# Token sums kept in fp32, weight sums regrouped, down products reordered and norm spreads put later in a one-core decoder trunk on Trainium2

## The chip, the cores and the metric

The kernel runs on one core of one Trainium2 chip. A core has TensorE (matrix products into the eight banks of PSUM), VectorE (DVE), ScalarE (ACT), GpSimd (POOL) and SyncE (SP), and 16 DMA engines that all queues share. The metric is the device time of one launch in microseconds, as the median over repeated runs.

## The reference

One layer of a decoder trunk over x of shape (1, 2048, 1024) in float32, conditioned by c:

```python
sh1, sc1, g1, sh2, sc2, g2 = jnp.split(mod, 6, axis=-1)      # mod = silu(c) @ w_ada + b_ada
h = rms_norm(x) * (1.0 + sc1) + sh1
x = x + g1 * token_mixer(h, ...)      # retention | HGRN2 | GLA heads, one in- and one out-projection
h = rms_norm(x) * (1.0 + sc2) + sh2
x = x + g2 * conv_ffn(h, ...)         # u = causal depthwise conv (width 3) of h @ w_up; (silu(gate) * val) @ w_down
return rms_norm(x) * final_gain
```

The token mixers run in chunks with a carried state; d_ff is 2816. Inputs are drawn from normal distributions, and some of the gains and biases are scaled up.

## The kernel before, in words

Every large product is made in float32 accuracy from two parts. `split` (L970 to L974) casts a tile to a rounded part `hi` on ScalarE (L972) and subtracts to get the remainder `lo` on VectorE (L973); `split3` (L239 to L243) then issues three matmuls, hi by hi, hi by lo and lo by hi.

The channel mixer works on pairs of blocks of 512 tokens, `s` = 0 and 1. Its two matrix products are done block by block in a 2 x 2 scheme of seven products instead of eight. They are numbered 1 to 7: each takes a sum or difference of weight blocks (the "weight sums") and one of token blocks (the "token sums"). In the up stage, `up_first` issues products 1, 2, 6, 5 and 7 of one feature tile `f` (22 of them), and `up_second` products 4 and 3 of the tile before, after product 1 of the next. X holds the running sum over 1, 6, 7 and 4, Y holds 2, Z holds 5 and then 3. In the down stage `down_stage` runs the seven products in an order of their own; each is 11 steps of 12 matmuls over four banks. X again gathers 1, 6, 7 and 4, and 2, 5 and 3 go to other banks. After a product its banks are read out into the residual rows y (L1421); once rows are whole, their squares go into a sum for the final norm (`sumsq`, L334 to L340).

Stages in order of time: a start-up; the mixers for four token blocks b = 0 to 3 (each with seven units of heads: h0, g, h1, h2, h3, r0, r1), with the output projection of block b interleaved into block b + 1; the up stage for s = 0, its down stage, and the same for s = 1.

Order of work. TensorE's instructions are issued in program order, which is written by hand: a small clock (`Clock`) counts TensorE's planned microseconds, and `clock.at(us, fn)` puts a later piece of work into the order once that much planned time has gone by. The other engines, and the DMA queues of SP and POOL, are put in order at compile time by a list scheduler that goes by priority (`tc.high_priority(offset=...)` moves a piece forward). On the chip each engine's queue is worked off in order.

Names that matter here:

- `rstd` (L312 to L332) makes a norm: matmuls with ones (the tile `ss..`, L319), three Newton steps on VectorE (L153 to L158), and after `gap` planned microseconds a broadcast by matmul (the tile `bc..`, L329), copied by ScalarE (L330).
- `norm1_stat(b)` squares block b's tokens and starts such a norm with gap 8.0; it is called ahead of unit h3 of the block before, and its result is used after that block's last unit.
- `weight_sums` (L872 to L886) makes weight sums from raw weights in the mixers, as background work, and stores them in DRAM (`sums`): all 11 of the down stage, and those of the odd tiles of the up stage, one job at a time from the list `jobs`, the last in block 3.
- `up_weights(s, f)` supplies the operands A of tile f. Where `sums` has them they are loaded into tiles `s` (tag t2s, two buffers) and split. Otherwise it loads the raw weights, makes four sums on VectorE (L1165, L1166, L1169, L1172), splits them, and stores them for the second pair.
- `early_sums(k)` runs in block 3, after the second to fifth unit: it makes the token sums for products 5, 6, 7 and 4 of pair 0, splits each (tile `eo`), and stores both parts in DRAM (`made`). It draws its tiles from the ring `xy` (four buffers of 1024 columns), from which the residual rows of the output projection and `weight_sums` draw too. `fetch_made(B, i)` loads both parts by DMAs on POOL's queue (L1025) into the operand tiles B.
- `out_finish` ends the last output projection: residual rows `x1` (L919), their squares, the norm n2, and the stores of x1 and of the normalised block.
- `down_norm(s, h, ...)` makes the final norm of half h, then scales the rows (L1286) and stores them by POOL. In pair 0 two of the first half's rows lie in t2s tiles. `last_product` replaces the last product of pair 1 and ends the kernel.
- PSUM rings: `acc` (four banks), `lev` (two), `late` (two).

Of the kernel before, what the change touches and what calls it, by code (L numbers as in the profile page):

```python
# [100 lines left out]
def trunk(ctx, tc, xT, vecs, cvec, cst, rope, msk, wada, win, walow, wgla, wout, wup, wdown, out):  # L101
# [30 lines left out]
    def late(name):  # L132
        return pt.tile([P, 512], F32, tag="tl", name=name, bufs=NTL)
# [199 lines left out]

    def sumsq(acc, x, k, name, sl=slice(0, TB), first=None):  # L334
        if k == 0 if first is None else first:
            S.activation(acc[:, sl], x[:, sl], AF.Square)
        else:
            sq = late(f"sq{name}{k}")
            S.activation(sq[:, sl], x[:, sl], AF.Square)
            V.tensor_tensor(acc[:, sl], acc[:, sl], sq[:, sl], op=ALU.add)  # L340
# [139 lines left out]
    def norm1_stat(b):  # L480
        acc = new_acc(f"n1_{b}")
        for k in range(KD):
            x = tmp(f"x{b}_{k}")
            nc.sync.dma_start(x[:], xT[b, :, k, :])
            sumsq(acc, x, k, f"n1_{b}_")
        bc1[b] = new_bc1(b)
        clock.at(22.0, rstd(acc, f"n1_{b}", bc1[b][:], lambda: done.add(("n1", b)), gap=8.0))

# [511 lines left out]
    def early_sums(k):  # L1000

        t1, t2 = (px.tile([P, SB], F32, tag="xy", name=f"es{k}_{i}", bufs=4) for i in range(2))
        b11, b12, b21, b22 = t1[:, 0:TB], t1[:, TB:SB], t2[:, 0:TB], t2[:, TB:SB]
        for dst, src in ((b11, h2d[0, k]), (b12, h2d[1, k]), (b22, h2d[1, k + 4]), (b21, h2d[0, k + 4])):
            nc.sync.dma_start(dst, src[:])

        def op(i, src):
            t = px.tile([P, SB], F32R, tag="xy", name=f"eo{k}_{i}", bufs=4)
            split(src, t[:, 0:TB], t[:, TB:SB])
            made[i, k] = pdr.tile([P, SB], F32, tag=f"made{i}_{k}", name=f"made{i}_{k}")  # L1010
            nc.sync.dma_start(made[i, k][:], t[:].bitcast(F32))
        V.tensor_tensor(b11, b12, b11, op=ALU.subtract)
        op(5, b11)
        V.tensor_tensor(b11, b22, b11, op=ALU.subtract)
        op(6, b11)
        V.tensor_tensor(b12, b22, b12, op=ALU.subtract)
        op(7, b12)
        V.tensor_tensor(b21, b21, b11, op=ALU.subtract)
        op(4, b21)

    def fetch_made(B, i):
        for k in range(4):
            B[i, k] = hc_tile(f"B0_{i}_{k}")
            for j, t in enumerate(B[i, k]):
                G.dma_start(t.bitcast(F32), made[i, k][:, j * TB:(j + 1) * TB])  # L1025

# [9 lines left out]
    for hi, lo, raw, i in W0.values():  # L1036
        keep(f"i{i}l", lo[:])
    jobs = [job for k in range(NF // 2) for job in (("d", k), ("u", 2 * k + 1))]
    for b in range(NB):
# [103 lines left out]

    def up_weights(s, f, A=None, rv=None, rg=None):

        nm = f"{s}_{f}"
        op = lambda i, src: up_op(A, s, f, i, src)
        half = lambda n, j: raw_half(wup[2 * f + n][:, 512 * j:512 * j + 512], f"r{n}{j}_{nm}")
        if A is None:
            A = {}  # L1150
            rv = half(0, 0), half(0, 1)
            op(1, rv[0])
            op(2, rv[1])
        s1, s2, s3, s4 = (t2s(f"s{i}_{nm}") for i in range(4))
        if ("u", f) in sums:
# [6 lines left out]
            return A  # L1162
        rg = rg or (half(1, 0), half(1, 1))
        d = new_sums(("u", f))
# [54 lines left out]
    def up_first(s, f, A, B, before, begun=None):  # L1219
        nm = f"{s}_{f}"  # L1220
        X, Y = begun or (acc_ps("X" + nm), lev_ps("Y" + nm))
        Z = acc_ps("Z" + nm)
# [38 lines left out]
    INTO = {1: [(0, 0)], 2: [(0, 0)], 6: [(1, 0)], 5: [(1, 0), (1, 4)], 7: [(1, 4)], 4: [(0, 4)], 3: [(1, 0)]}  # L1261
    WHOLE = {2, 7, 4, 3}

# [15 lines left out]
    def down_norm(s, h, y, acc, bc, bank=None):  # L1279
# [11 lines left out]
        def then():  # L1291
            for i, m in enumerate(order):
                clock.at(2.0 * i, lambda m=m: scale(m))
        clock.at(7.0 if h else 10.0, rstd(acc, f"n3_{b}", bc[:], then, bank=bank, gap=4.5 if h else 8.0))

# [16 lines left out]
    def last_product(s, y, acc):  # L1312
# [56 lines left out]
        whole = slice(0, TB)  # L1369
        banks = [lev_ps(f"dL{p}") for p in range(2)]  # L1370
        run([b[:] for b in banks], (0, 1), whole, M512)
# [12 lines left out]
    def down_stage(s, between):  # L1384
# [4 lines left out]
        accs = [px.tile([P, TB], F32, tag=t, name=f"n3a{s}_{h}", bufs=1) for h, t in enumerate(("ssacc", "bc2"))]  # L1389
        for i in (1, 2, 6, 5, 7, 4, 3):  # L1390
            if i == 3 and s == NSB - 1:
                last_product(s, y, accs[1])
                return
            ps = X
            if i in (2, 5, 3):
                ps = [f(f"dY{s}_{i}_{p}") for p, f in enumerate((lev_ps, lev_ps, late_ps, late_ps))]
            for k in range(NF // 2):
# [12 lines left out]
                for p in range(4):  # L1410
# [3 lines left out]
                    adv(3 * M512)  # L1414
                if between and i in (7, 4, 3):
                    next(between, None)
            y = y or down_rows(s)
            with tc.high_priority(offset=HOT):
# [4 lines left out]
                if i in WHOLE:  # L1423
                    h, m = INTO[i][0]
                    for p in range(4):
                        sumsq(accs[h], y[h, m + p], m + p, f"n3_{s}_{h}_", first=i in (2, 7) and p == 0)
            if i == 4:
# [4 lines left out]

    rg0 = raw_half(wup[1][:, 0:512], "r10_0_0"), raw_half(wup[1][:, 512:1024], "r11_0_0")
    fetch_made(B, 6)
# [5 lines left out]
    with tc.high_priority(offset=100):  # L1440
        out_finish(NB - 1, lambda: up_weights(0, 0, A, (rv0[:, 0:512], rv0[:, 512:1024]), rg0), out_begun)
    for i in (7, 4):
# [120 lines left out]
```

## Time and profile before

| | us |
|---|---|
| Runs before: median of 3 (lowest to highest) | 2555.14 (2554.24 to 2556.89) |
| The profiled execution's own time | 2559.62 |
| Its span | 2557.9 |
| TensorE busy | 2486.8 (97%) |
| VectorE busy | 1952.3 (76%) |
| ScalarE busy | 1133.5 (44%) |

A busy time is the share of the span in which an engine worked; it says nothing about which engine set the pace in a given stretch. What an engine waited for is read from the table of waits: the engine and line that waited, the engine, tile and line whose end released it, the total in microseconds, how often, and the longest. In the order of time a bracket shows the idle time ahead of an instruction and its releaser. In the windows table each row has a stretch, its length, the busy time of PE, PEld (weight loads), DVE, ACT and POOL with instruction counts, the clock granted to TensorE (1.00 is full), the share of the DMA engines in use, and GB/s. In this profile the mixers reach to about 1240 us, the first up stage to 1688, the first down stage to 1904, the second up stage to 2332, and the second down stage to the end.

### The profile page before, as it was taken

To read this page: it belongs to the slowest core of one execution; us is meant where nothing else is said; L and a number is where in the kernel's file an instruction comes from. 1 tells how busy PE (TensorE), PEld (TensorE's weight loads), DVE (VectorE), ACT (ScalarE), POOL (GpSimd) and SP (SyncE) were. 2 spreads that over 40 slices of the span, in tenths; PEclk is the share of its full clock that TensorE was granted. 3 is DMA by queue.
4 is the path that set the end of the run, shared out by engine and by line. 5 is a ranking of instruction groups with operands and counts; after the bars stand their busy time and mean duration, and the time that the engine had idled before them with its cause. 6 is when DMAs were issued, how large, how long until landed. Compare 5 with 4: busy or idle time off the path is not lost.

```text
span 2557.9 us, 37048 instructions
## 1 busy us (share of the span) xinstructions
PE 2486.8 (97%) x13146; PEld 2117.1 (83%) x13146; DVE 1952.3 (76%) x3568; ACT 1133.5 (44%) x1906; POOL 163.2 (6%) x287
## 2 busy tenths in 40 slices
PE   5999999999999999999899999999989999999998
PEld 4889888888888888898788888888878888888887
DVE  7788986868677676787588888887677778778666
ACT  3433434423443235433254545455444455455442
POOL 1000000000000000000200000000001001000000
PEclk9999999999999999999999999999999999999999
DMA  8454576675687846886745444477675544447653
GB/s 300 164 196 165 204 265 209 224 259 196 221 326 244 276 168 223 299 295 231 284 168 173 150 149 158 149 275 248 209 222 169 154 147 145 154 137 257 215 193 127
DMA packets 229337, 533.84 MB, mean 209 GB/s; under 512 B 25216, under 2 KB 28320, under 8 KB 229152
## 3 DMA queue, kind: packets, MB, share of 16 engines
q1 hardware_dynamic: 224672, 516.80, 59.1%
q0 software_dynamic: 4480, 14.68, 1.6%
q8 instruction: 103, 1.69, 0.3%
q14 instruction: 82, 0.67, 0.1%
HBM read 397.69 MB, written 133.69 MB: 208 GB/s over the span
## 4 chain that ended last, share of the span: by engine, by line
PE 60%; DMA 4%; DVE 4%; ACT 1%; issue 1%; SPq 0%; DVEq 0%; ACTq 0%
PE X L241 6%; PE X L242 6%; PE X L243 6%; PE Z L242 3%; PE Z L241 3%; PE Z L243 3%; PE dX L242 3%; PE dX L241 3%; PE dX L243 3%; PE dY L242 2%; PE dY L241 2%; PE dY L243 2%; PE Y L242 2%; PE Y L243 2%; PE Y L241 2%; PE lvh L610 1%
## 5 line engine op out<-in xcount | busy, mean ns | idle before, releaser
L241 PE MATMUL X<-B,A 128*128 128x512 f32 x572 | 223.1, 390 | 1.4 <-ACT u L1246 1.4
L243 PE MATMUL X<-B,A 128*128 128x512 f32 x572 | 222.6, 389 | 0.0
L242 PE MATMUL X<-B,A 128*128 128x512 f32 x572 | 222.5, 389 | 0.0
L973 DVE TENSOR_TENSOR dA<-rd,dA 128x512 fp32r<-128x512 f32 x154 | 106.0, 689 | 90.6 <-ACT dA L972 89.6
L972 ACT CAST dA<-rd 128x512 fp32r<-128x512 f32 x154 | 95.7, 621 | 145.2 <-PE dY L243 45.6
L973 DVE TENSOR_TENSOR A<-s,A 128x512 fp32r<-128x512 f32 x176 | 120.7, 686 | 45.2 <-ACT A L972 44.8
L241 PE MATMUL psvgh<-hvgh,ha 128*128 128x256 f32 x480 | 142.0, 296 | 0.0
L972 ACT CAST A<-s 128x512 fp32r<-128x512 f32 x176 | 108.6, 617 | 70.1 <-PE Z L243 46.8
L242 PE MATMUL psvgh<-lvgh,ha 128*128 128x256 f32 x480 | 137.0, 285 | 0.0
L243 PE MATMUL psvgh<-hvgh,ha 128*128 128x256 f32 x480 | 136.9, 285 | 0.0
L241 PE MATMUL dX<-dB,dA 128*128 128x512 f32 x352 | 136.9, 389 | 0.0
L242 PE MATMUL dX<-dB,dA 128*128 128x512 f32 x352 | 136.9, 389 | 0.0
L243 PE MATMUL dX<-dB,dA 128*128 128x512 f32 x352 | 136.9, 389 | 0.0
L241 PEld LDWEIGHTS X<-B,A 128*128 128x128 f32 x572 | 107.4, 188 | 24.3 <-ACT u L1246 2.2
L243 PEld LDWEIGHTS X<-B,A 128*128 128x128 f32 x572 | 107.4, 188 | 22.3
L610 PE MATMUL lvh<-qbh,kh 128*128 128x128 f32 x896 | 123.0, 280 | 2.9 <-DVE nw L157 2.3
L242 PEld LDWEIGHTS X<-B,A 128*128 128x128 f32 x572 | 107.4, 188 | 22.1
L610 PEld LDWEIGHTS lvh<-qbh,kh 128*128 128x128 f32 x896 | 117.0, 194 | 9.7 <-issue 3.8
L241 PE MATMUL Z<-B,A 128*128 128x512 f32 x308 | 120.4, 391 | 0.0
L242 PE MATMUL Z<-B,A 128*128 128x512 f32 x308 | 120.3, 391 | 0.0
L243 PE MATMUL Z<-B,A 128*128 128x512 f32 x308 | 120.3, 391 | 0.0
L973 DVE TENSOR_TENSOR dB<-rb,dB 128x512 fp32r<-128x512 f32 x154 | 105.5, 686 | 10.0 <-ACT dB L972 9.8
(461 smaller groups left out, 7054.8 us busy)
## 6 DMA issues: line engine op xcount, KB each, us to landing
gs<-yv SPq DMA_DIRECT2D x154, 256.0 KB, 2.8
rb<-gs SPq DMA_DIRECT2D x154, 256.0 KB, 4.1
r<-wup SPq DMA_DIRECT2D x141, 256.0 KB, 3.3
s<-sumsu SPq DMA_DIRECT2D x132, 256.0 KB, 3.0
wada<-wada SPq DMA_DIRECT2D x48, 512.0 KB, 5.0
rd<-sumsd SPq DMA_DIRECT2D x88, 256.0 KB, 3.9
rd<-wdown SPq DMA_DIRECT2D x66, 256.0 KB, 3.8
x<-xT SPq DMA_DIRECT2D x64, 256.0 KB, 5.7
```

Source lines behind the costliest of these rows:

```text
L241: T.matmul(ps, lhs[0], rhs[0], start=first, stop=False, skip_group_check=more)
L242: T.matmul(ps, lhs[0], rhs[1], start=False, stop=False, skip_group_check=more)
L243: T.matmul(ps, lhs[1], rhs[0], start=False, stop=last, skip_group_check=more)
L610: T.matmul(ps[:, c * P:(c + 1) * P].rearrange("p (h n s) -> p h n s", h=2, s=s), kq[rs, c * P:(c + 1) * P], rhs, start=True, stop=True)
L972: S.copy(hi, src)
L973: V.tensor_tensor(lo, src, hi, op=ALU.subtract)
```

## The change

- The token sums of pair 0 are stored in fp32 (256 KB each instead of 512 KB of two parts). `fetch_made` loads each into a staging tile (tag t2k, four buffers) and splits it there.
- The last background job makes the sums of up tile 0 instead of tile 21. The first pair's tile 0 loads its sums; tile 21 makes its own. The early loads of tile 0's gate weights go.
- The down products run in the order 1, 2, 6, 7, 4, 5, 3 instead of 1, 2, 6, 5, 7, 4, 3. Product 3 of pair 0 goes to four `acc` banks, the first two banks of the last product too; the first X of the second up stage takes a `late` bank. Squares are summed after 2, 4, 5 and 3 instead of 2, 7, 4 and 3, and those after product 3 use t2k tiles.
- The gap of norm1 grows from 8 to 14, that of the second half's final norm from 4.5 to 8.

```diff
-        clock.at(22.0, rstd(acc, f"n1_{b}", bc1[b][:], lambda: done.add(("n1", b)), gap=8.0))
+        clock.at(22.0, rstd(acc, f"n1_{b}", bc1[b][:], lambda: done.add(("n1", b)), gap=14.0))
...
-    def sumsq(acc, x, k, name, sl=slice(0, TB), first=None):
+    def sumsq(acc, x, k, name, sl=slice(0, TB), first=None, room=None):
...
-            sq = late(f"sq{name}{k}")
+            sq = (room or late)(f"sq{name}{k}")
...
     def early_sums(k):
...
         def op(i, src):
-            t = px.tile([P, SB], F32R, tag="xy", name=f"eo{k}_{i}", bufs=4)
-            split(src, t[:, 0:TB], t[:, TB:SB])
-            made[i, k] = pdr.tile([P, SB], F32, tag=f"made{i}_{k}", name=f"made{i}_{k}")
-            nc.sync.dma_start(made[i, k][:], t[:].bitcast(F32))
-        V.tensor_tensor(b11, b12, b11, op=ALU.subtract)
-        op(5, b11)
-        V.tensor_tensor(b11, b22, b11, op=ALU.subtract)
-        op(6, b11)
+            made[i, k] = pdr.tile([P, TB], F32, tag=f"made{i}_{k}", name=f"made{i}_{k}")
+            nc.sync.dma_start(made[i, k][:], src)
+        t3 = px.tile([P, SB], F32, tag="xy", name=f"es{k}_2", bufs=4)
+        s5, s6 = t3[:, 0:TB], t3[:, TB:SB]
+        V.tensor_tensor(s5, b12, b11, op=ALU.subtract)
+        op(5, s5)
+        V.tensor_tensor(s6, b22, s5, op=ALU.subtract)
+        op(6, s6)
         V.tensor_tensor(b12, b22, b12, op=ALU.subtract)
         op(7, b12)
-        V.tensor_tensor(b21, b21, b11, op=ALU.subtract)
+        V.tensor_tensor(b21, b21, s6, op=ALU.subtract)
         op(4, b21)

     def fetch_made(B, i):
         for k in range(4):
-            B[i, k] = hc_tile(f"B0_{i}_{k}")
-            for j, t in enumerate(B[i, k]):
-                G.dma_start(t.bitcast(F32), made[i, k][:, j * TB:(j + 1) * TB])
+            x = t2k(f"hm{i}_{k}")
+            G.dma_start(x[:], made[i, k][:])
+            B[i, k] = split(x[:], *hc_tile(f"B0_{i}_{k}"))
...
-    jobs = [job for k in range(NF // 2) for job in (("d", k), ("u", 2 * k + 1))]
+    jobs = [job for k in range(NF // 2) for job in (("d", k), ("u", 2 * k + 1 if k < 10 else 0))]
...
-    def up_weights(s, f, A=None, rv=None, rg=None):
+    def up_weights(s, f, A=None):
...
-        if A is None:
-            A = {}
+        begun, A = A, A or {}
+        if not begun:
...
-        rg = rg or (half(1, 0), half(1, 1))
+        rg = half(1, 0), half(1, 1)
...
-        X, Y = begun or (acc_ps("X" + nm), lev_ps("Y" + nm))
+        X, Y = begun or ((late_ps if s and not f else acc_ps)("X" + nm), lev_ps("Y" + nm))
...
-    WHOLE = {2, 7, 4, 3}
+    WHOLE = {2, 4, 5, 3}
+    TURN = (1, 2, 6, 7, 4, 5, 3)
...
-        clock.at(7.0 if h else 10.0, rstd(acc, f"n3_{b}", bc[:], then, bank=bank, gap=4.5 if h else 8.0))
+        clock.at(7.0 if h else 10.0, rstd(acc, f"n3_{b}", bc[:], then, bank=bank, gap=8.0))
...
-        banks = [lev_ps(f"dL{p}") for p in range(2)]
+        banks = [acc_ps(f"dL{p}") for p in range(2)]
...
-        for i in (1, 2, 6, 5, 7, 4, 3):
+        for i in TURN:
...
-            if i in (2, 5, 3):
+            if i == 3:
+                ps = [acc_ps(f"dX{s}_3_{p}") for p in range(4)]
+            elif i in (2, 5):
...
-                if between and i in (7, 4, 3):
+                if between and i in TURN[4:]:
...
-                    h, m = INTO[i][0]
+                    h, m = INTO[i][-1]
                     for p in range(4):
-                        sumsq(accs[h], y[h, m + p], m + p, f"n3_{s}_{h}_", first=i in (2, 7) and p == 0)
+                        sumsq(accs[h], y[h, m + p], m + p, f"n3_{s}_{h}_", first=i in (2, 5) and p == 0, room=t2k if i == 3 else None)
...
-    rg0 = raw_half(wup[1][:, 0:512], "r10_0_0"), raw_half(wup[1][:, 512:1024], "r11_0_0")
     fetch_made(B, 6)
     fetch_made(B, 5)
...
-        out_finish(NB - 1, lambda: up_weights(0, 0, A, (rv0[:, 0:512], rv0[:, 512:1024]), rg0), out_begun)
+        out_finish(NB - 1, lambda: up_weights(0, 0, A), out_begun)
```

## The prediction

> **What bounds the kernel.** I read the page first, then TensorE's own waits stretch by stretch, then the windows table for the granted clock, and last the chain and the order of time around each wait.
>
> ```profile
> span 2557.9 us, 37048 instructions
> PE 2486.8 (97%) x13146; PEld 2117.1 (83%) x13146; DVE 1952.3 (76%) x3568; ACT 1133.5 (44%) x1906; POOL 163.2 (6%) x287
> ```
>
> TensorE is busy 2486.8 of 2557.9 us. No edit changes a product, so all there is to win is its 71.1 us of idleness and what runs at a lowered clock. TensorE's instructions stand in an order fixed by hand, so whatever it waits for stops everything behind. These are the waits near the edits: first the mixers (0 to 1250), then 1180 to 1300, then 1860 to 1960.
>
> ```profile
> PE bcn L329 <- DVE rsn L158: 5.4, 2, 2.7
> PE pshfh L241 <- DVE sgg L531: 2.1, 1, 2.1
> ...
> PE ssn L319 <- DVE san L340: 4.2, 1, 4.2
> PE y L243 <- DMA lwo<-kepto7l: 1.6, 1, 1.6
> PE y L241 <- DMA hwo<-kepto7h: 1.1, 1, 1.1
> PE bcn L329 <- DVE rsn L158: 0.8, 1, 0.8
> ...
> PE Y L241 <- DVE y L1421: 2.6, 1, 2.6
> PE ssn L319 <- DVE n3a L340: 2.4, 1, 2.4
> PE X L241 <- ACT m L1233: 1.7, 1, 1.7
> ```
>
> They add to 21.9 us. The windows table has start:end, length, then busy us of PE, PEld, DVE, ACT, POOL, then the granted clock:
>
> ```profile
> 820.00:840.00 20.00, 17.26 (x105) 15.69 (x105) 13.32 (x34) 4.58 (x8) 0.00 (x0) 0.91 0.70 242
> 1030.00:1040.00 10.00, 8.15 (x39) 6.29 (x40) 6.90 (x16) 1.91 (x7) 0.00 (x0) 0.83 0.77 279
> 1240.00:1300.00 60.00, 52.26 (x219) 42.10 (x218) 40.45 (x69) 27.06 (x46) 13.79 (x28) 0.91 0.79 283
> 1868.00:1904.00 36.00, 33.62 (x150) 27.62 (x149) 29.94 (x57) 15.31 (x27) 3.25 (x6) 0.95 0.72 224
> 1904.00:1934.00 30.00, 25.74 (x114) 20.74 (x113) 23.11 (x45) 14.00 (x26) 6.64 (x13) 0.94 0.62 205
> ```
>
> Around each wait the clock is lowered as well: (1 - clock) x length is 1.8, 1.7, 5.4, 1.8 and 1.8 us. So a wait costs more than its own length, and the five windows give a second ledger of 12.5 us.
>
> **Norm spread in the mixers (gap 8 to 14).** The sums of norm1 (ssn) go to VectorE's Newton steps, and TensorE comes back for the broadcast (bcn) one gap later.
>
> ```profile
> 812.67 1.05 PE ssn L319 x8
> 826.39 1.26 PE bcn L329 x8
> ```
>
> The answer took 13.7 us; TensorE was there 2.7 us early, 11.0 us after the sums. Six more microseconds of projections between make it 17.0, so both 2.7 us waits go. What is moved is eight small matmuls and one copy on ScalarE; the norm isn't used before the block's last unit is through. Gain 5.4 of wait and half of the window's 1.8 of clock (the dots' wait just before shares it): 6.3. Bounds: 2.7 (one wait comes back as another wait on VectorE) to 7.2.
>
> **Token sums in fp32.** Sixteen casts and sixteen subtractions leave the last mixer block and its sixteen stores halve (one tile of 512 columns for two).
>
> ```profile
> 1020.06 4.05 DMA made<-eo
> 1024.19 0.62 ACT eo L972
> ACT eo L972 <- DMA made<-eo: 8.7, 5, 2.8
> ```
>
> The chain reads: a store frees an eo tile, the cast that waited for it stands at the head of ScalarE's queue, behind it the gate's sigmoid, then sgg on VectorE, for which TensorE's 2.1 us wait is put down. That cast is gone. The new code takes three of the four xy tiles at once instead of two and one, so loads can start later; the residual rows and weight sums that use the same ring are queued behind. Gain 3.0 out of 2.1 + 1.7 = 3.8; bounds -2.1 (as long as the wait removed, should the tile ring make a new one) to 3.8.
>
> **The way into the up stage.** Here the cost is put down. The sixteen splits come back, after a load into four staging tiles:
>
> ```profile
> L972 ACT CAST A<-s 128x512 fp32r<-128x512 f32 x176 | 108.6, 617 | 70.1 <-PE Z L243 46.8
> L973 DVE TENSOR_TENSOR dB<-rb,dB 128x512 fp32r<-128x512 f32 x154 | 105.5, 686 | 10.0 <-ACT dB L972 9.8
> B<-made POOLq DMA_DIRECT2D x24, 256.0 KB, 7.9
> DMA to landing us min/median/max: 2.6/5.1/9.0
> 1241.72 4.23 POOL L1025 DMA_DIRECT2D B<-made  x8 [22.62 <-PE oTr L550]
> 1263.63 0.39 PE L241 MATMUL X<-B,A 128*128 128x512 f32 x1
> 1263.86 0.39 PE L242 MATMUL X<-B,A 128*128 128x512 f32 x1
> ```
>
> That is 16 x 0.617 = 9.9 us of ScalarE and 16 x 0.686 = 11.0 us of VectorE; four sum additions (2.7) leave, to f = 21. VectorE goes from 40.45 to about 48.7 of 60 us: it fits, if the operands arrive. The split tiles come free at 1241.72, as before. In the worst order each group of four loads waits for the four splits ahead of it: 7.9 + 2.7 = 10.6 us a group. Operand 6 is then ready at 1244.4, 5 at 1255.1, 7 at 1265.7, 4 at 1276.3, 3 at 1286.9. A product is twelve matmuls of 0.23, 2.7 us. Less the waits for the weight pair (2.7) product 6 starts at 1260.9, 5 at 1263.6, 7 at 1266.4, 4 (after one product of the next tile) at 1271.8, 3 at 1274.5. The last is 12.4 late, and takes the place of the earlier lateness. So the bad end is 7.7 of waits gone less 12.4, -4.7. The good end is all waits and clock, 7.7 + 5.4 = 13.1.
>
> By the Trainium skill's DMA: Bandwidth & Descriptors (anatomy of one DMA, SWDGE path) a load costs about 2.0 us plus bytes over 436 GB/s, an estimate of 2.6 us here; the trace's fastest landing agrees, its median under load is double. By that figure a group takes 5.3 us, nothing is late, and this part would be no less than 7.7.
>
> What speaks for a gain is the cause of the 4.2 us wait:
>
> ```profile
> 1254.47 12.85 DMA sumsu<-s
> 1267.42 0.69 DVE L1172 TENSOR_TENSOR s<-rv,s 128x512 f32<-128x512 f32 x1 [5.58 <-DMA sumsu<-s]
> 1180.82 0.32 SPq L886 DMA_DIRECT2D sumsu<-wsu  x1
> ```
>
> The fourth sum of f = 0 needs a tile whose store took 12.85 us, and blocks the last residual row and its square behind it. Now f = 0's sums are stored by the mixers (the last such store is issued at 1180.82) and only loaded; no store stands in VectorE's way. Bytes fall too: POOL's operand loads halve (one 256 KB load for two), and on SP two loads and four stores become five loads. On SP the third and fourth of these wait for a t2s tile until an earlier sum is split, with the residual stores and the next weights queued behind. I give back 4.2 and 0.8, and keep the 2.7 on the weight pair and the 5.4 of clock as the price of the splits: gain 5.0.
>
> **Down products.** With 4 ahead of 5, the first half's norm runs during 5, not during the last product. Also 7 now follows 6 in the same banks, so 7 can't begin on a bank before VectorE has read it. The old 4 after 7 was such a place, and cost nothing: the first bank is read from 1836.45 on, while the last matmuls of the other three run. The rows of the stage before:
>
> ```profile
> 1836.45 2.72 DVE L1421 SCALAR_TENSOR_TENSOR y<-dX,mod,y 128x512 f32<-128x512 f32 x4
> 1896.21 4.06 DVE L1286 SCALAR_TENSOR_TENSOR y<-y,vec,n3b 128x512 f32<-128x512 f32 x6
> 1899.98 1.05 SPq L1160 DMA_DIRECT2D s<-sumsu  x2
> 1904.85 0.62 ACT L972 CAST A<-s 128x512 fp32r<-128x512 f32 x1 [5.79 <-DMA s<-sumsu]
> 1903.63 0.39 PE L241 MATMUL X<-B,A 128*128 128x512 f32 x1
> 1908.20 2.72 DVE L1421 SCALAR_TENSOR_TENSOR y<-dY,mod,y 128x512 f32<-128x512 f32 x4
> ```
>
> Two output rows of the first half sit in the tiles that the next weight sums need. They are scaled at 1896, so the sums load at 1899.98, the cast waits 5.79, VectorE behind it, and the last product's rows are read out at 1908.20 instead of soon after 1903.63, where the product had ended. Y waits for these banks, X for m, the norm's sums for the squares. With that norm a product (132 matmuls of 0.23, 30 us) earlier the tiles are free; Y and X no longer take the banks of product 3 (now acc, for which Z comes three products of 2.7 us later), and the squares' tiles (now t2k) no longer those of m. Product 5's eight read-outs and four squares (12 x 0.7 = 8.4 us) move into the last product, and eight scalings (5.9) leave it. Gain 6.7 of waits (2.4 + 2.6 + 1.7) and half of 3.6 of clock: 8.5; bounds 0 (no loss: the matmuls stay, a blocked load goes) to 10.3. Should VectorE still be late at the end, Z waits as Y did, 2.6.
>
> ```profile
> 1300.00:1640.00 340.00, 340.00 (x1502) 281.62 (x1501) 285.99 (x359) 172.06 (x252) 25.29 (x72) 1.00 0.47 157
> ```
>
> **At nothing:** f = 21's four additions (2.7 us in a tile of seven products, 19 us, of which VectorE is busy 286 parts in 340; uncovered, 2.7 once); the gap 4.5 to 8 at the second half's norm (no wait there now, and X of the new stage only holds a late bank); the tail, whose last rows now end on other banks (within 0.5 either way).
>
> **Sum.** 6.3 + 3.0 + 5.0 + 8.5 = 22.8 us. The profiled execution took 2559.62, its span and 1.7 around it; the median of the runs is 2555.14, 4.48 less. 2559.62 - 22.8 - 4.48 = 2532.3. The ceiling, 7.2 + 3.8 + 13.1 + 10.3 = 34.4, gives 2520.7.
>
> **Rivals.** *Only the waits come back.* The slowed stretches might have another cause than the waits.
>
> ```profile
> 1032.38 0.43 PE pshfh L242
> 510.00:520.00 10.00, 7.33 (x62) 7.12 (x62) 7.89 (x28) 1.47 (x4) 0.00 (x0) 1.00 0.89 306
> ```
>
> After the 2.1 us wait matmuls stand 0.43 apart instead of 0.23, which speaks against it. For it: the first bcn wait lies in 510 to 520, and the clock there is 1.00. Then 5.4 + 2.1 + 5.0 + 6.7 = 19.2, 2535.9. The Trainium skill's TensorE: Matmul & The Clock Gate (Part 1) has the clock halve after an idle window of some 3.4 us; by that only the 4.2 us wait would slow anything, and this rival would hold; the 0.43 does not agree with it.
>
> *The splits come in series.* The way in costs 4.7, the token sums give nothing, one of the two bcn waits comes back: 2.7 + 0 - 4.7 + 8.5 = 6.5, so 2548.7. For it: ScalarE and VectorE take work in order, and 7.9 us is the median landing there. Against: the DMA bytes fall.
>
> *Slower: a load at the head of the queue.* If splits are queued ahead of the residual rows in VectorE's order, each of the four groups behind the first shows its 7.9 us to TensorE: 31.6 of waits for the old 7.7, -23.9. With 5.4 + 3.0 + 8.5 elsewhere that is +7.0, 2562.1. It decides from (16.9 + 7.7) / 7.9, over three exposed groups. The 5.58 us that VectorE lost to s L1172 shows the mechanism; against it, the first tiles can be filled ahead of 1241.
>
> **Chances.** Forecast 0.60, only the waits 0.10, series 0.20, slower 0.10. A measurement tells about 0.2%, 5.1 us, so faster means under 2550.0. The series case lies around that line, half on each side: faster 0.60 + 0.10 + 0.10 = 0.80, same 0.10, slower 0.10. The range runs from 2521 (the ceiling) to 2550, leaving out the slower case and half of the series.
>
> **What would show it.** bcn L329 in the mixers without a wait on rsn; no made<-eo behind a cast; no sumsu<-s behind a sum at the stage's start, but casts of B from a staging tile, and X or Z waiting on such a split if the series is right; no Y wait at the second up stage, its weight casts done ahead of the stage; windows there at clock 1.00. Wrong would be: waits of over 12 us between 1240 and 1300, or the end of the first down stage as late as before.

## The result, and the profile after

The changed kernel takes 2541.9 us (median of 4 runs, 2538.74 to 2545.59), the kernel before in the same runs 2555.83 (2554.24 to 2556.89). The ratio is 0.9938 with a 95% interval of 0.9918 to 0.9959: 15.8 us faster. Two later sets, on two chips, gave 0.9939 (0.9926 to 0.9952) and 0.9931 (0.9914 to 0.9948). The forecast was 2532.3, a gain of 22.8 us, in a range of 2521 to 2550. So the sign and the range held, and the size was seven microseconds too good.

The profiled execution of the changed kernel is the fastest of its runs (2538.74) and that of the kernel before the slowest of its own (2559.62). The pair differs by 20.9 us, five more than the ratio gives. The pair is used to see what went and what came; sizes are taken from the timed runs and from the two further profiles of the changed kernel.

The head of the page, after:

```profile
span 2537.0 us, 36995 instructions
PE 2478.0 (98%) x13146; PEld 2106.8 (83%) x13146; DVE 1949.7 (77%) x3568; ACT 1134.1 (45%) x1906; POOL 151.4 (6%) x271
```

TensorE's idle time fell from 71.1 to 59.0 us. That is 12.1 of the 20.9; the other 8.8 is busy time, and since no matmul was removed it is the same work at a higher clock. In the two further profiles the idle time falls by about as much, 12.8 and 10.8, but the busy time by 2.1 and 1.5 only. The waits after, first from 1180 to 1310, then from 1640 to 1965 (waited total, times, longest):

```profile
PE Z L242 <- DVE B L973: 4.0, 2, 3.7
PE X L241 <- ACT hB L972: 0.3, 1, 0.3
PE Z L241 <- ACT B L972: 0.3, 1, 0.3
...
PE dX L242 <- DVE dB L973: 2.2, 2, 1.8
PE dX L241 <- DVE y L1424: 1.6, 1, 1.6
PE X L241 <- ACT u L1246: 0.7, 1, 0.7
PE Z L242 <- DVE B L973: 0.4, 1, 0.4
PE Z L241 <- ACT B L972: 0.2, 1, 0.2
```

All nine waits that the prediction listed are gone. In the mixers no new line of over a microsecond stands in their place. At the way into the up stage 7.7 us of waits became 4.6, nearly all one wait of Z for a split of B. In the down stage and the stage behind it 7.4 (0.7 of it for u, which stays) became 5.1. The same five windows as before:

```profile
820.00:840.00 20.00, 20.00 (x112) 17.24 (x111) 11.86 (x24) 5.82 (x9) 0.00 (x0) 1.00 0.93 325
1030.00:1040.00 10.00, 9.75 (x72) 8.65 (x70) 8.83 (x20) 1.54 (x2) 0.00 (x0) 1.00 0.86 304
1240.00:1300.00 60.00, 55.47 (x227) 43.84 (x227) 50.90 (x83) 36.96 (x60) 7.50 (x16) 0.91 0.68 229
1868.00:1904.00 36.00, 34.15 (x155) 28.06 (x154) 28.37 (x56) 16.59 (x30) 0.72 (x2) 1.00 0.69 219
1904.00:1934.00 30.00, 29.38 (x133) 23.85 (x132) 26.51 (x37) 16.28 (x26) 5.88 (x10) 1.00 0.66 213
```

Four have full clock now. The way in has 0.91 as before: its slow stretch belongs to the new wait.

How far the kernel is ahead of the kernel before at five marks in time, taken from the order of TensorE's instructions in three profiles of the changed kernel (the first shown above, and the two from the sets E and H below), all against the one profile of the kernel before:

| mark | first | E | H |
|---|---|---|---|
| last matmul on oTr (end of the mixers' heads) | 14.2 | 8.3 | 8.4 |
| product 6 of f = 0 | 19.0 | 13.2 | 13.0 |
| Y of f = 1 | 16.6 | 10.1 | 10.1 |
| first down stage starts | 16.6 | 10.1 | 10.0 |
| Y of f = 1, second pair | 21.4 | 14.9 | 13.8 |

So what repeats is: mixers 8.4, then 4.8 gained up to product 6, 3.0 lost again up to Y of f = 1, and 4 to 5 gained over the down stage and the way out of it. The first profile's further 6 us lie in the mixers, and are clock: over the windows of 10 us up to 1240, (1 - clock) x length adds to 10.2 us before, 1.7 in the first profile after and 8.5 in that of E.

### The profile page after: what moved, and what is told of

Its sections match the earlier page's. It is cut to its first block, busy times and chain, and to the rows that moved or that the text cites. A ratio compares the mean times of both kernels' runs of the same rounds, so it can differ in the third digit from the quotient of the medians.

```text
span 2537.0 us, 36995 instructions
## 1 busy us (share of the span) xinstructions
PE 2478.0 (98%) x13146; PEld 2106.8 (83%) x13146; DVE 1949.7 (77%) x3568; ACT 1134.1 (45%) x1906; POOL 151.4 (6%) x271
## 4 chain that ended last, share of the span: by engine, by line
PE 59%; DMA 4%; DVE 4%; issue 1%; ACT 1%; SPq 0%; DVEq 0%; ACTq 0%; POOLq 0%
PE X L241 6%; PE X L242 6%; PE X L243 6%; PE Z L242 3%; PE Z L243 3%; PE Z L241 3%; PE dX L241 3%; PE dX L242 3%; PE dX L243 3%; PE lvh L610 2%; PE Y L242 2%; PE Y L243 2%; PE Y L241 2%; PE psqkvgr L243 1%; PE psqkvgr L241 1%
## 5 line engine op out<-in xcount | busy, mean ns | idle before, releaser
L242 PE MATMUL dX<-dB,dA 128*128 128x512 f32 x396 | 154.3, 390 | 2.2 <-DVE dB L973 2.2
L241 PE MATMUL dX<-dB,dA 128*128 128x512 f32 x396 | 154.2, 389 | 1.6 <-DVE y L1424 1.6
L243 PE MATMUL dX<-dB,dA 128*128 128x512 f32 x396 | 154.1, 389 | 0.0
```

The lines of the kernel that those rows point to most:

```text
L241: T.matmul(ps, lhs[0], rhs[0], start=first, stop=False, skip_group_check=more)
L242: T.matmul(ps, lhs[0], rhs[1], start=False, stop=False, skip_group_check=more)
L243: T.matmul(ps, lhs[1], rhs[0], start=False, stop=last, skip_group_check=more)
```

## The experiments

**Set A to D: each part alone.** All four stand beside the same kernel before (30 runs, median 2561.57).

*A, the gap alone.*

```diff
-        clock.at(22.0, rstd(acc, f"n1_{b}", ..., gap=8.0))
+        clock.at(22.0, rstd(acc, f"n1_{b}", ..., gap=14.0))
```

> The kernel before with one edit: the gap of norm1 from 8 to 14. Theory (waits, and the clock around them): both 2.7 us waits of bcn on rsn go and the clock around the second recovers, -6.3 us, 2549. Rival (the waits only change place, since the same Newton steps still stand in VectorE's queue): within 2 us of before, with new waits of lvh, oh or og on VectorE in the same two blocks. Rival (the clock lowers after other waits as well): -5.4 us or less, with low clock windows still at 500 and 820.

Measured: 2555.56 us (6 runs), ratio 0.9974 (0.9963 to 0.9985), 6.7 us, with an interval from 3.8 to 9.5. No bcn L329 stands among the waits of the mixers. The forecast of 6.3 holds.

*B, the token sums alone* (`early_sums` and `fetch_made` of the change).

> The kernel before with the token sums stored in fp32 and split once loaded, nothing else. Theory: the 2.1 us wait of pshfh in the last mixer block and its slow clock go (-3 to -4 us), while the way into the up stage gets slower by some us, since the sixteen splits stand beside the old sums of tile 0: a wait of X or Z on a split of 2 to 12 us. Sum between -3 and +8 us. Rival (the DMA bytes were the cause at the way in): no wait on a split, hwo and lwo waits gone, -6 us or more.

Measured: 2557.25 (12 runs), 0.9987 (0.9975 to 0.9999), 3.3 us. The waits for the weight pair and for ssn went, though this kernel still makes and stores tile 0's weight sums at the way in. In their place, from 1180 to 1310:

```profile
PE Z L242 <- DVE B L973: 4.1, 4, 2.8
PE X L242 <- DVE B L973: 1.1, 1, 1.1
PE Z L241 <- ACT B L972: 0.8, 2, 0.7
```

So the splits' own cost is 6.0 us of waits. That the others went tells where they came from. The store of a weight sum that took 12.85 us before takes 2.7 here, and the load of the weight pair 4.8 instead of 8.0: between 1230 and 1262 us only 6 loads of token sums are issued, where it was 20. So the slow store came with that burst of loads.

*C, the weight sums alone* (tile 0 in the mixers, tile 21 not).

> The kernel before with the weight sums of up tile 0 made in the mixers and those of tile 21 in the up stage, nothing else. Theory: the fourth sum no longer stands behind a store, so the 4.2 us wait of ssn and the 0.8 of bcn at the way into the up stage go, and part of the slow clock: -5 to -8 us, and nothing at tile 21. Rival (ScalarE or VectorE now waits for the load of the sums instead): 0 to -2 us, the ssn wait still there.

Measured: 2562.59 (12 runs), 0.9998 (0.9987 to 1.0009): nothing, where 5 to 8 us were expected. The waits from 1180 to 1310:

```profile
PE y L241 <- DMA hwo<-kepto7h: 7.6, 1, 7.6
PE X L242 <- DMA lB<-made: 1.9, 1, 1.9
```

The 4.2 us on ssn is gone, and TensorE waits 7.6 us for a load of the output projection's weight pair, where it was 1.1: this load takes 14.5 us to land. The blocked store was one way to be late there; the loads are another.

*D, the down stage alone* (`TURN`, `WHOLE`, the banks, the squares' tiles).

> The kernel before with the down stage's edits alone (order 1 2 6 7 4 5 3, banks, squares, gap 8 for the second half's norm). Theory: the waits of ssn, Y and X at the end of the first down stage go (6.7 us) with their slow clock, but product 7 waits some 1.6 us for the read-out of product 6 and two small waits on dB come: -5 to -7 us, all of it after 1770. Rival (the new waits give back most): -2 us or less. The way into the up stage as before.

Measured: 2560.14 (12 runs), 0.9988 (0.9975 to 1.0001), 3.1 us. From 1640 to 1965:

```profile
PE dX L241 <- DVE y L1424: 1.5, 1, 1.5
PE Z L241 <- ACT B L972: 1.4, 1, 1.4
PE dX L242 <- DVE dB L973: 0.7, 1, 0.7
```

The 6.7 us of Y, ssn and m went; 3.6 us of other waits came, so 3.1 are left. The measured 3.1, where 5 to 7 were expected, has an interval from 0.3 slower to 6.4 faster, so that the two agree to the tenth is chance.

**Set E: the whole, and two parts together.** Beside 18 runs of the kernel before (median 2563.09), as were the kernel of F and the first of G.

*E, the changed kernel again.*

> The changed kernel itself, beside the four single parts' kernel before. The four parts alone gave 6.7, 3.3, 0 and 3.1 us against the kernel before, 13.1 together. If the parts don't touch each other, this one gains 13 (12 to 14.5). If the halved loads of the token sums also feed the weight sums (the weight sums alone made a 7.6 us wait for a load at the way in, which the whole change doesn't show), it gains 16 to 19: more than the sum of its parts. If the slow stretches come back by chance and not from the waits, the clock will be at 0.993 to 0.996 as in the earlier runs of it, and its profile will show other slow windows than 1250 to 1270, with the gain still in that span.

Measured: 2544.78 (5 runs), 0.9939 (0.9926 to 0.9952), 15.6 us. The four parts alone give 13.1, so up to 2.5 come from the parts together. The intervals are about that wide, which settles no interaction by itself.

*Token sums and weight sums together.*

> Token sums in fp32 and the weight sums of tile 0 made in the mixers, both, and nothing else of the change. Alone they gave 3.3 and 0. My theory: the weight sums alone gave nothing because a load of the weight pair (hwo) stood behind the 512 KB groups of operand loads at the way in (a wait of 7.6 us); with these halved, that wait is gone, and the two together give 5 to 9 us, with neither the ssn wait of 4.2 nor the hwo wait; Z waits 3 to 4 us for a split of B instead. The rival: the two simply add, 3.3 us (2 to 4.5), and the hwo wait or another of its size stands there.

Measured: 2556.78 (12 runs), 0.9981 (0.9970 to 0.9992), 4.9 us. By time alone this can be told neither from the rival's 3.3 nor from the 5 to 9 of the theory. The profile tells more; its first rows from 1180 to 1310:

```profile
PE Z L242 <- DVE B L973: 4.1, 3, 3.5
PE y L241 <- DMA hwo<-kepto4h: 1.0, 1, 1.0
```

The 7.6 us load wait of C does not come: the same load lands in 4.1 us, and again only 6 loads of token sums are issued between 1230 and 1262, where C has 22. So the token sums' edit takes the burst of loads away, which the weight sums' edit alone left in place; the split of B is what remains. Whether the halved bytes do it, or the four staging tiles, which spread the loads in time, is not separated.

**F: why Z waits at the way in.** In the changed kernel the loads of operand 5 on POOL's queue, the two splits of operand 6 that end last, operand 5's casts, a square on VectorE, operand 5's first splits, and the product that waits:

```profile
1229.43 1.14 POOL L1024 DMA_DIRECT2D hm<-made  x2 [12.72 <-DMA r<-wup]
1239.45 1.14 POOL L1024 DMA_DIRECT2D hm<-made  x2 [8.89 <-ACT sqn L339]
...
1238.25 1.28 DVE L973 TENSOR_TENSOR B<-hm,B 128x512 fp32r<-128x512 f32 x2
...
1235.96 1.12 ACT L972 CAST B<-hm 128x512 fp32r<-128x512 f32 x2
1245.32 0.62 ACT L972 CAST B<-hm 128x512 fp32r<-128x512 f32 x1 [2.55 <-DMA hm<-made]
...
1247.55 0.69 DVE L340 TENSOR_TENSOR san<-san,sqn 128x512 f32<-128x512 f32 x1 [2.19 <-ACT sqn L339]
...
1250.62 1.29 DVE L973 TENSOR_TENSOR B<-hm,B 128x512 fp32r<-128x512 f32 x2
...
1251.37 0.50 PE L242 MATMUL Z<-B,A 128*128 128x512 f32 x1 [3.67 <-DVE B L973]
```

Z needs operand 5, and stands until the first split of it has run, at 1250.62. In the trace's semaphores that split belongs to the tile whose load was issued at 1229.43. Its data had landed at 1233.50 and was cast at 1235.96; its split then stood 14 us in VectorE's queue, behind residual rows, squares and splits of weight sums. For one of these squares VectorE stood 2.19 us, and here a late load comes in by way of ScalarE. Two of the four staging tiles hold operand 6 until VectorE has split it, at 1238.25 to 1239.5. Only then are the last two loads of operand 5 issued (1239.45; the bracket's releaser is inferred, the tiles' last reader is that split). They land 5.8 and 6.3 us later, ScalarE waits 2.55 us for the first of them, and the square stands behind that cast. The experiment moves the loads and the splits ahead:

```diff
-    fetch_made(B, 6)
-    fetch_made(B, 5)
+    with tc.high_priority(offset=200):
+        fetch_made(B, 6)
+        fetch_made(B, 5)
```

> The changed kernel with the loads and splits of operands 6 and 5 of the token sums put 200 steps ahead in the planner's order, so that VectorE takes the four splits of 6 and of 5 ahead of the weight sums of tile 0. My theory: the 3.7 us wait of Z on a split of B, and the slow clock behind it (3.6 + 1.5 us lost in 1250 to 1270), come from the staging tiles of operand 6 being freed late (its last two splits ended at 1238.25, behind residual rows), so that the loads of operand 5 were late. Then this wait falls under 1 us, and the kernel is 3 to 7 us faster than the changed one. The rival: loads are late because the transfers themselves are slow there (5 to 8 us under load); then the wait stays at 3 to 4 us, or turns into one on a weight sum's split (X or Z on A), and the time is the same within 2.

Measured: 2541.01 (6 runs), 0.9928 (0.9912 to 0.9944), 18.5 us. From 1180 to 1310:

```profile
PE bcn L329 <- DVE rsn L158: 3.0, 1, 3.0
PE X L243 <- DVE A L973: 1.6, 1, 1.6
PE X L242 <- DVE lB L973: 1.2, 1, 1.2
```

The wait of Z is gone, so its cause is shown to lie in the order, not in the speed of the loads: operand 5's last two still take 5.5 and 4.9 us to land. The theory had the order right but put the late load first; the split that Z waited for had its data long before. Weight sums and a norm, now behind the splits, are late in turn, as the rival had it for the weight sums. From product 6 to Y of f = 1 it took 25.0 us instead of 29.5. The waits add to 5.8 us, in E's profile to 5.3, so this is not waiting saved: the granted clock from 1240 to 1300 is 1.00, in E 0.91. The whole kernel's gain over E (2.4 by the means, where 3 to 7 were expected) is inside the error of these runs.

**G: why product 7 waits in the down stage.** The changed kernel around the end of product 6, VectorE and ScalarE:

```profile
1760.15 0.69 DVE L1119 TENSOR_TENSOR hr_0b<-hr_0b,hr_0b 128x512 f32<-128x512 f32 x1 [2.20 <-DMA hr_0b<-h2d]
1760.87 0.62 ACT L972 CAST hB<-hr_0b 128x512 fp32r<-128x512 f32 x1 [3.73 <-DVE hr_0b L1119]
1762.13 2.72 DVE L1424 SCALAR_TENSOR_TENSOR y<-dX,mod,y 128x512 f32<-128x512 f32 x4
```

A sum for the next stage (`up_inputs`), written in the program at product 4, was put by the planner ahead of product 6's read-outs. Its load is late, VectorE stands for 2.20 us, and the read-outs that free product 7's banks stand behind it. First a coarse test, in which the operands are prepared a whole product later:

```diff
-                if between and i in TURN[4:]:
+                if between and i in TURN[5:]:
```

> The changed kernel with the next stage's operands prepared from product 5 on, not from product 4 on (TURN[5:] in place of TURN[4:]); the planner then no longer pulls them ahead of product 6's read-outs. My theory: product 7's wait of 1.6 us on that read-out comes from VectorE standing behind a sum of such an operand that waits for its load, 2.2 us; then the wait at 1763 is under 0.3 us and the first down stage up to product 4 is 1.3 to 1.6 us shorter. What it costs: the same 20 steps in 22 places instead of 33 crowd into the last two products, where waits on a split of dB already stood at 2.2 us: 0 to 4 us more there. In all -1.5 to +3 us against the changed kernel. The rival: product 7 waits for the read-out itself (0.69 us from the last matmul on a bank, four in a row); then the wait stays 1 to 1.6 us with nothing ahead of the read-outs on VectorE.

Measured: 2552.81 (6 runs), 0.9967 (0.9955 to 0.9979), 8.5 us under the kernel before and 7 us worse than E. The wait at 1763 is gone, which bears the cause out. The price was mis-sized, I had 0 to 4:

```profile
PE X L241 <- ACT m L1233: 8.2, 1, 8.2
...
1903.01 0.68 DVE L1126 TENSOR_TENSOR hr_3b<-hr_7b,hr_3b 128x512 f32<-128x512 f32 x1
1903.93 0.59 ACT L1233 COPY m<-X 128x512 f32<-128x512 f32 x1 [2.08 <-DVE hr_3b L1126]
```

The last of the sums now lies 12 us into the next stage, which starts at 1890.72. The copy m, for which X waits, takes its tile from the same ring of three (t2m) as the staged operands, and that tile came free only when this sum had read it. Then a fine test: that one sum alone is queued behind the read-outs.

```diff
             b11, b12, b22 = ...
-            V.tensor_tensor(b11[:], b12[:], b11[:], op=ALU.subtract)
+            if k == 0:
+                with tc.issue_after(read[0]):       # read[0]: the last read-out of product 6
+                    V.tensor_tensor(b11[:], b12[:], b11[:], op=ALU.subtract)
+            else:
+                V.tensor_tensor(b11[:], b12[:], b11[:], op=ALU.subtract)
...
```

> The changed kernel with one instruction moved: VectorE's first sum of the next stage's operands (L1119 of hr_0b), which waited 2.20 us for its load ahead of product 6's read-outs, now stands right behind them (four places later in its queue); all else on VectorE keeps its order. My theory: the 1.6 us wait of product 7 falls to under 0.4 us and the clock stays as it was; the kernel is 1 to 3 us faster than the changed one (0.6% and a further 0.04 to 0.12% under the kernel before), without the wait of 8.2 us for m that the coarse shift of all steps brought. The rival: the wait is the read-outs' own time; then it stays over 1 us and the time is the same.

Measured: 2541.6 (6 runs), 0.9926 (0.9906 to 0.9945), beside 11 runs of the kernel before at 2557.87. Product 7 no longer waits, and no wait for m has come. VectorE's order there:

```profile
1765.41 2.72 DVE L1430 SCALAR_TENSOR_TENSOR y<-dX,mod,y 128x512 f32<-128x512 f32 x4
1769.85 0.69 DVE L1123 TENSOR_TENSOR hr_0b<-hr_0b,hr_0b 128x512 f32<-128x512 f32 x1
```

So the wait was VectorE's queue and not the read-outs' own time. What it is worth can't be told from these runs: its ratio is 0.0013 better than E's, with 0.002 and 0.0013 to each side. The changed kernel's own wait there was 1.6, 0.6 and 1.2 us in its three profiles.

**H: towards a better version.** First (beside the run just told) a version in which a split of operand 5 and one of a weight sum take turns:

```diff
-    fetch_made(B, 6)
-    fetch_made(B, 5)
+    with tc.high_priority(offset=200):
+        fetch_made(B, 6)
+    with tc.high_priority(offset=60):
+        fetch_made(B, 5)
...
-    ... gap=8.0 if b < NB - 1 else 4.5))        # norm2
+    ... gap=8.0))
```

together with the sum behind the read-outs.

> The changed kernel with three edits: the loads and splits of operand 6 put 200 steps ahead in the planner's order and those of operand 5 60 steps (so that on VectorE a split of operand 5 and one of a weight sum take turns); the first sum behind product 6's read-outs, as in the run before; gap 4.5 to 8 at the last half's norm2. My theory: with all of operand 5 put ahead the stage to f = 1 was 4.5 us shorter, but product 6 waited 1.6 us for a weight sum's split and the norm's broadcast 3.0 us; taking turns and the longer gap remove both. Then 1180 to 1310 shows under 2 us of waits, and the kernel is 4 to 8 us faster than the changed one, 19 to 24 us under the kernel before. The rival: the loads at the way in take 5 to 8 us each whatever their order, and what is taken from one wait comes back in the next (on A, lB or hB); then it is within 3 us of the changed kernel.

Measured: 2541.21 (6 runs), 0.9925 (0.9908 to 0.9942): the same as without the turns. In the waits the rival was right: Z still waits 1.8, and ssn 1.7, hwo 1.4 and hB 1.3 came, where under 2 us in all were expected. The time can't decide: 19.2 us under the kernel before lies at the lower end of the expected 19 to 24, and 3.6 more than E gained on another chip. Then both operands ahead, with the longer gap and the sum behind the read-outs, and the changed kernel beside it on the same chip:

> As the last run, but with both operands 6 and 5 put 200 steps ahead (as in the first run with them ahead), the first sum behind product 6's read-outs, and gap 8 at the last half's norm2. My theory: taking turns had each wait come back elsewhere (Z 1.8, ssn 1.7, hB 1.3); all of 5 ahead cost 1.6 on a weight sum and 3.0 on the norm's broadcast, of which the gap takes the 3.0. From product 6 of f = 0 to Y of f = 1 then takes 24 to 26 us (changed kernel 28.8 and 29.5), and the kernel is 2 to 5 us under the changed kernel on the same chip. The rival: it is within 2 us of the changed kernel, as the waits move on to the splits behind.

> The changed kernel again, beside the run above on the same chip. If the parts add as before, it is 13 to 18 us under the kernel before; its mean granted clock will again be 0.003 to 0.004 above that of the kernel before.

Measured, beside 11 runs of the kernel before at 2560.55: 2537.91 (6 runs), 0.9909 (0.9892 to 0.9926), and the changed kernel 2545.47 (6 runs), 0.9931 (0.9914 to 0.9948). The means differ by 6.1 us, with an error of about 4, where 2 to 5 were expected. This version beats both kernels. The first waits from 1180 to 1310, and the window, first of this version and then of the changed kernel beside it:

```profile
PE X L243 <- DVE A L973: 1.9, 1, 1.9
PE Z L241 <- ACT B L972: 1.1, 1, 1.1
...
1240.00:1300.00 60.00, 55.34 (x247) 44.51 (x246) 53.71 (x90) 40.93 (x68) 8.08 (x16) 1.00 0.77 250
```

```profile
1240.00:1300.00 60.00, 54.83 (x224) 42.66 (x223) 50.30 (x85) 37.23 (x63) 7.32 (x16) 0.91 0.70 232
```

The longer gap took the 3.0 us on bcn away. Waits of 0.6 to 1.9 us are left, and the clock is full: TensorE issues 247 matmuls in these 60 us instead of 224. From product 6 to Y of f = 1 it is 24.3 us instead of 29.3. Again hardly any of this is waiting saved: the waits from 1180 to 1310 add to 5.2 us here and to 5.7 in the changed kernel, whose longest is 3.1. What the new order does is to break one long wait into short ones, and behind these the clock stayed up in this profile; in the version with the turns, whose longest wait is 1.7, it was 0.94.

## Why the prediction was right, and where it was off

**The gap: right.** 6.3 forecast, 6.7 measured alone.

**Token sums in the mixers: right.** The casts that waited for stores are gone and so is the wait of pshfh; the mixers as a whole are 8.4 us shorter in the two profiles of the changed kernel whose clock resembles that of before, where 6.3 + 3.0 = 9.3 was forecast.

**The way in: a term mis-sized, 5.0 forecast, about 1.8 measured** (4.8 gained up to product 6, 3.0 lost up to Y of f = 1). The step that failed is "I give back 4.2 and 0.8, and keep the 2.7 on the weight pair and the 5.4 of clock as the price of the splits". The wait on the weight pair went too, and the price of the splits was not the old slow stretch alone. That stretch cost 5.4 and stayed at 5.4 (0.91 of 60 us both times), and beside it the splits put a new wait of TensorE of 4.0. The forecast had asked whether VectorE's busy time fits ("it fits, if the operands arrive"), and not where in its queue the splits would stand. The worst-order reckoning let every split run as soon as its load had landed. In the trace the split that Z waited for ran 17 us after that, behind other work; a late load of a later tile made this worse by way of ScalarE. The series rival was thus half right: Z did wait on a split of B, but for 3.7 us and for its place in the queue, not for a series of loads that ends 12.4 late. Its price of a load was too high as well: the sixteen loads took 2.8 to 6.3 us, half of them no more than 3.8, not 7.9. (The forecast's row 2.6/5.1/9.0 mixes the loads with the sixteen stores of 512 KB; the loads alone have 2.8/6.2/9.0.) The reason I gave for a gain, the store of 12.85 us that blocks VectorE, was true of the trace but not the root. In C the store went, and the load of the weight pair took its place; in B the store stayed and became quick, because the burst of token-sum loads was gone.

**The down products: a term mis-sized, 8.5 forecast, 3.1 alone and 4 to 5 in the whole.** All three waits went, as said. The step that failed is product 7 after 6: it was judged by the old 4 after 7, where VectorE was free and the change of product "cost nothing". Here VectorE was not free, because the planner had put a sum with a late load ahead of the read-outs. G shows it by moving that sum. The splits of dB in product 3 that are late by 0.7 to 2.2 us were not foreseen at all. The rows ahead of them, in the changed kernel's first profile, show the same mechanism a second time:

```profile
1856.92 0.69 DVE L1119 TENSOR_TENSOR hr_3b<-hr_3b,hr_3b 128x512 f32<-128x512 f32 x1 [3.48 <-DMA hr_3b<-h2d]
...
1859.80 5.36 DVE L1424 SCALAR_TENSOR_TENSOR y<-dY,mod,y 128x512 f32<-128x512 f32 x8
```

VectorE stands 3.48 us for the load of another such sum, and product 5's eight read-outs and product 3's splits stand behind it; in the profiles of D, E and H's changed kernel it is 3.5 to 3.8 us at the same place. In the coarse test of G, which moves these sums, VectorE is busy all the time from 1855 to 1865 and no split of dB is late. No run moves this one sum alone.

**At nothing: right.** The stretch from Y of f = 1 to the down stage takes 398.1 us before and after in both pairs of blocks (399.7 once, in the second pair of H's profile of the changed kernel, where the clock fell), so f = 21's four additions cost nothing. The second down stage has the same waits before and after.

**The sum.** 0.9 too much in the mixers, 3.2 at the way in and about 3.7 at the down stage make the 7 to 8 us that the forecast of 22.8 lies over the measured 15.6.

**The clock rival fell, though its number lay nearer.** With waits alone coming back, no busy time could have gone, and it went in all three profiles (8.8, 2.1 and 1.5 us). In the two later sets the mean granted clock of the timed runs rose from 0.990 to 0.993 and 0.994. The rival's 19.2 lies nearer to the measured 15.6 than the forecast's 22.8, but that is luck: its 19.2 were all waits, and the idle time fell by 10.8 to 12.8 us. By stage, as TensorE's idle time and busy time less than in the profile before (each pair is E, H):

| stage | idle forecast | idle | clock forecast | busy |
|---|---|---|---|---|
| mixers | 7.5 | 7.3, 6.4 | 1.8 | 1.0, 2.1 |
| up to Y of f = 1 | 5.0 | 2.7, 2.6 | 0 | -1.0, -0.9 |
| first down stage to Y of f = 1, second pair | 6.7 | 2.7, 1.8 | 1.8 | 2.1, 1.9 |

So it is the waits that fell short, by what the new waits at the way in and in the down stage took back, and the clock came out near its terms, but for 1 us at the way in. What the clock gave over many runs is less sure. Over the timed runs of the last set, mean time x (1 - mean granted clock) is 25.2 us for the kernel before, 16.1 for the changed one and 13.5 for the version of H; of the 17.1 us between the first two means that would be 9.0. But this product counts slow time in which TensorE stood idle too: in the profiles of the kernel before and of H's changed kernel it falls by 5.2, and TensorE's busy time by 1.5. Which wait slows what stays open. Between 500 and 510 the clock is lowered in every profile but the first of the changed kernel. Its waits from 440 to 515:

```profile
PE lvh L610 <- DVE nw L157: 1.3, 1, 1.3
PE oTg L550 <- DVE og L544: 1.2, 1, 1.2
PE ssn L319 <- ACT doth L602: 0.5, 1, 0.5
```

The same kernel's second profile, where the clock there was 0.83, has the same two first lines and 0.3 in the third. So the same waits cost 1.7 us of clock in one execution and none in the other. So the half of the clock that the forecast added where a wait went came out about right over a stage of these two profiles, and can't be counted on at one place.

**The slower rival** needed more than three exposed groups of loads. TensorE showed one wait of that kind, 3.7 us long, and its load had landed.

## What to carry to other kernels

When work is taken out of one stage and given to another, ask not only whether the engine has the time, but where in its queue the work will stand: here a split whose data had landed 17 us before held up TensorE. Look up as well which ring its staging tiles come from and who must run before they are freed: a load can be late by its predecessor's last reader, and an engine that waits for it at the head of its queue holds up everything behind. Waits that can't be removed may be worth breaking up: in H they add to almost the same, and the stretch is 5.0 us shorter. When a wait is to go, list what the same place would wait for next, and take it from the trace of the place itself, since a transition that was free elsewhere tells little of an engine's queue here. Compare two profiles only after their granted clocks have been compared; a quarter of the difference of a pair can be that.

## What the hardware showed unexpectedly

The clock drops to exactly half, for multiples of about 3.4 us, and after waits shorter than that. The kernel before, in windows of 1 us (after the stretch and its length comes PE's busy time; the granted clock is the third column from the end):

```profile
1030.00:1031.00 1.00, 0.00 (x0) 0.00 (x0) 1.00 (x2) 0.18 (x2) 0.00 (x0) 1.00 0.94 209
1031.00:1032.00 1.00, 0.15 (x1) 0.18 (x2) 1.00 (x5) 0.46 (x3) 0.00 (x0) 1.00 1.05 348
1032.00:1033.00 1.00, 1.00 (x3) 0.77 (x4) 0.90 (x3) 1.00 (x3) 0.00 (x0) 0.55 0.99 369
1033.00:1034.00 1.00, 1.00 (x4) 0.77 (x3) 0.88 (x2) 0.28 (x2) 0.00 (x0) 0.50 0.97 381
1034.00:1035.00 1.00, 1.00 (x4) 0.81 (x3) 0.01 (x1) 0.00 (x0) 0.00 (x0) 0.50 1.07 438
1035.00:1036.00 1.00, 1.00 (x8) 0.42 (x9) 0.00 (x0) 0.00 (x0) 0.00 (x0) 0.74 1.02 412
```

The lost clock adds to 0.45 + 0.50 + 0.50 + 0.26 = 1.71 us, so 3.4 us at half speed, behind a wait of 2.1 us. A wait of 3.67 in the changed kernel was followed by 10.2 us at half speed, 5.1 lost: the slowing cost more than the wait. The Trainium skill's TensorE: Matmul & The Clock Gate (Part 1) gives a free-running window of some 3.4 us for this: the length agrees with these rows; that a whole idle window is needed does not, since 2.1 us sufficed. A short wait does not always do it: the 3.0 us on bcn in F had full clock behind it. Over the fourteen profiles, after the first 100 us, all fifteen waits of TensorE of more than 3.0 us had a slow stretch begin in them or within 1.7 us of their end; of the shorter ones some had and some had not. A stretch that comes in one execution and stays out in another would fit a window that runs freely, and it goes with the spread of one kernel's times: the 30 runs of the kernel before beside A to D lie between 2554.4 and 2571.99 with a granted clock from 0.987 to 0.993, and over them 0.001 of clock goes with 2.2 us.
